# The same instruction streams behind an empty, closed tile context, instead of inside two critical sections of an open one

## The chip, the cores and the metric

The kernel runs on one core of a Trainium2 chip. The core has five engines with an instruction stream each: PE (matrix multiply), DVE (vector), ACT (scalar), POOL (general purpose) and SP (here it only issues DMAs and waits). The metric is the device time of one execution in microseconds. The kernel before was timed three times: 210.34, 210.49 and 210.49, median 210.49 us.

## What is computed

```python
batch, m, k, n = 16, 512, 1024, 768        # everything float32
x: [16, 512, 1024]   weight: [1024, 768]   bias: [768]   residual: [16, 512, 768]
out = np.matmul(x, weight) + bias + residual
```

As one product it has 8192 rows, cut into 64 tiles of 128 rows. Per tile the contraction of 1024 is eight steps of 128, and the 768 output columns are a part of 512 and one of 256.

## The kernel before, in words

**The work.** SP loads x and residual in pieces of several tiles into two large SBUF tensors (`X`, 16 tiles deep, and `R`, 32 tiles deep) and stores finished tiles from `R`. ACT casts an x tile to bf16 (`XB`). PE transposes it as four 128x128 blocks of 32-bit words (L335) into PSUM (`PT`), DVE copies that to SBUF (`XT`), and PE multiplies (weights L353, matmul L342) into one of three PSUM tiles (`PO`). DVE adds PSUM into the residual (L286), and POOL adds the bias (L286). Four tiles near the end are transposed by ACT and DVE instead (L297 to L331). At the start the weights are loaded, cast and kept, and PE runs dummy products (L397) on a zeroed tile before the first data land.

**The order.** Nothing is scheduled by a planner. The code calls `op(engine, emit, reads, writes)`, which appends to a list in `Program.add` (L59), and `ORDER` (L36) and `HEAD_ORDER` (L30) fix by hand what SP issues and how the first three tiles are interleaved. `Program.emit` (L72) works out from reads and writes which instruction must wait for which, gives each DMA a landing semaphore (`landed_0` and so on, L118), and emits each engine's stream with explicit waits (L134). For PE, the middle 54 tiles are a loop of nine turns with six tiles each (`Fori`, L160); its first instruction is placed at a fixed slot of a fetch block (`head_slot`).

**Around the streams.** The kernel runs inside `with TileContext(nc)` (L493). Memory comes from two tile pools, and semaphores from the tile context. The streams are emitted in a critical section (L461); behind them SP waits for the landings of all stores but the last four (L463). A second critical section, on SP alone (L465), has the waits for those four. What the tile framework puts around a critical section is not in the kernel's text: a NOP on SP at the start (L461), for which all engines wait in a branch (L493); after the first section a drain on each engine and SP's waits for them (L461); after the second a branch, an event, a drain and a NOP on SP (L493, L465); and at the end of the context two barriers of all engines with a clearing of semaphores between them (L493). A barrier is a drain on each engine that counts up a semaphore, POOL's wait for four of them, POOL's release, and each engine's wait for that release. One more such barrier stands at the very start (L482), from the making of the program itself, behind four small memsets on POOL.

Of the kernel before, what the change touches and what calls it, by code (L numbers as in the profile page):

```python
# [11 lines left out]
P = 128  # L12
QUAD = 32
# [26 lines left out]
 ('r', 2, 6, 16), ('s', 1, 0, 16), ('x', 3, 0, 6), ('r', 3, 0, 7), ('x', 3, 6, 16),  # L40
 ('r', 3, 7, 16), ('s', 2, 0, 16), ('s', 3, 0, 10), ('s', 3, 10, 13),
 ('s', 3, 13, 15), ('c', 3, 15, 0), ('c', 3, 15, 1)]
OUTSIDE = 4
LAST = [(0, 512), (512, 256)]


class Program:

    def __init__(self, tc):
        nc = tc.nc
        self.nc, self.tc = nc, tc
        self.engines = {"pe": nc.tensor, "dve": nc.vector, "act": nc.scalar, "pool": nc.gpsimd, "sp": nc.sync}
        self.ops, self.writer, self.readers = [], {}, {}
        self.form, self.kind = [], []

    def add(self, eng, emit, rd=(), wr=(), dma=False, kind=None):  # L59
        n, ops = len(self.ops), self.ops  # L60
        deps = {self.writer[k] for k in (*rd, *wr) if k in self.writer and (eng != "pe" or ops[self.writer[k]][0] != eng)}
        for k in wr:
            deps.update(d for d in self.readers.get(k, ()) if ops[d][0] != eng or ops[d][3])
        for k in rd:
            self.readers.setdefault(k, set()).add(n)
        for k in wr:
            self.writer[k], self.readers[k] = n, set()
        self.ops.append((eng, emit, deps - {n}, dma))
        self.form.append((tuple(rd), tuple(wr)))
        self.kind.append(kind or f"done_{eng}")  # L70

    def emit(self, ends, turns):  # L72

        ops, known = self.ops, {e: {} for e in self.engines}
        lane, count, snap, waits, slots, slot = [], {}, [], [], [], {}  # L80
        for n, (eng, _, deps, dma) in enumerate(ops):
            mine = (n, 0) if dma else (eng, count.setdefault(eng, 0) + 1)
            if not dma:
                count[eng] += 1
            seen = known[eng]
            need = {}
            for d in deps:
                f, i = lane[d]
                if seen.get(f, -1) < i and i > need.get(f, (-1, 0))[0]:
                    need[f] = (i, d)  # L90
            need = {
                f: (i, d) for f, (i, d) in need.items()
                if not any(snap[d2].get(f, -1) >= i for g, (_, d2) in need.items() if g != f)
            }
            for f, (i, d) in need.items():
                for g, v in (*snap[d].items(), (f, i)):
                    if seen.get(g, -1) < v:
                        seen[g] = v
            waits.append([d for _, d in need.values()])
            lane.append(mine)  # L100
            if dma:
                free = [i for i, used in enumerate(slots) if seen.get(used[-1], -1) >= 0]
                if not free:
                    free = [len(slots)]
                    slots.append([])
                slot[n] = free[0], len(slots[free[0]]) + 1
                slots[free[0]].append(n)
            own = dict(seen)
            own[mine[0]] = mine[1]
            snap.append(own)  # L110
        body = [[n for n in range(a, b) if ops[n][0] == "pe"] for a, b in zip(turns, turns[1:])]
        for same in zip(*body, strict=True):
            assert len({self.form[n] for n in same}) == 1, [self.form[n] for n in same]
        told = {d for w in waits for d in w}
        told |= {n for same in zip(*body) if told & set(same) for n in same}
        told |= {n for n, k in enumerate(self.kind) if not k.startswith("done_")}
        sems = {k: self.tc.alloc_semaphore(k) for k in dict.fromkeys(self.kind) if k != "done_sp"}
        landings = [self.tc.alloc_semaphore(f"landed_{i}") for i in range(len(slots))]  # L118
        total, mark = dict.fromkeys(sems, 0), {}
        for n, (eng, _, _, dma) in enumerate(ops):  # L120
            if dma:
                mark[n] = (landings[slot[n][0]], 16 * slot[n][1])
            elif n in told:
                total[self.kind[n]] += 1
                mark[n] = (sems[self.kind[n]], total[self.kind[n]])

        def put(n, e):
            ins = ops[n][1](e)
            if ops[n][3]:
                ins.then_inc(mark[n][0], 16)  # L130
            elif n in told:
                ins.then_inc(mark[n][0], 1)

        def straight(todo):  # L134
            for n in todo:
                e = self.engines[ops[n][0]]
                for d in waits[n]:
                    e.wait_ge(*mark[d])  # L138
                put(n, e)

        pe = self.engines["pe"]
        straight(n for n, op in enumerate(ops) if op[0] != "pe" or n < turns[0])
        at = {}
        for same in zip(*body):
            for j, n in enumerate(same):
                for d in waits[n]:
                    at.setdefault(same[0], {}).setdefault(self.kind[d], {})[j] = mark[d][1]
        first, step = {}, {}
        order = [(n, k, w) for n in body[0] for k, w in at.get(n, {}).items()]
        for k in dict.fromkeys(k for _, k, _ in order):  # L150
            mine = [w for _, g, w in order if g == k]
            n_w = len(mine)
            assert all(len(w) == len(body) for w in mine), (k, mine)
            flat = [w[j] for j in range(len(body)) for w in mine]
            assert flat == list(range(flat[0], flat[0] + len(body) * n_w)), (k, flat)
            first[k] = flat[0]
        reg = {k: pe.alloc_register(f"count_{k}") for k in first}
        for k, r in reg.items():
            pe.reg_mov(r, first[k])
        with self.nc.Fori(0, len(body), 1, engines=OrderedEngineSet([pe.engine]), head_slot={pe.engine: 32}):  # L160
            for n in body[0]:
                for k in at.get(n, {}):
                    pe.wait_ge(sems[k], reg[k])
                    pe.reg_add(reg[k], reg[k], 1)
                put(n, pe)
        straight(n for n, op in enumerate(ops) if op[0] == "pe" and n >= turns[-1])
        return [mark[n] for n in ends]
# [3 lines left out]
def kernel(  # L171
# [8 lines left out]
    nc = tc.nc  # L180
# [11 lines left out]
    out_d = out2d.rearrange("(S p j) n -> S p j n", p=P, j=J)  # L192
    w_d = weight.rearrange("(q p e) n -> p q e n", p=P, e=2)

    sb = ctx.enter_context(tc.tile_pool(name="sb", bufs=1))
    ps = ctx.enter_context(tc.tile_pool(name="ps", bufs=1, space=bass.MemoryType.PSUM))

    def fixed(pool, name, n, shape, dt):
        return [pool.tile(shape, dt, name=f"{name}", tag=f"{name}{i}", bufs=1) for i in range(n)]

    (X,) = fixed(sb, "x_tile", 1, [P, XR, K], FP32)
    (R,) = fixed(sb, "ro", 1, [P, RR, N], FP32)
    XB = fixed(sb, "xb", XB_N, [P, K], BF16)
    XT = fixed(sb, "xt", XT_N + 1, [P, n_q, P, 2], BF16)
    XD = fixed(sb, "xd", 2, [P, 2, n_q, P // QUAD, 2 * QUAD], BF16)
# [9 lines left out]
    prog = Program(tc)  # L215
# [5 lines left out]
    def dma(dst, src, rd, wr):  # L221
        op("sp", lambda e: e.dma_start(out=dst, in_=src), rd, wr, dma=True)  # L222
# [6 lines left out]
    stores = []  # L229

    def pump():
        while queue:
# [18 lines left out]
            queue.pop(0)  # L251
            t0, nj = J * S + j0, j1 - j0
            if kind == "b":
                dma(bias_row.rearrange("(g p) n -> g p n", p=QUAD)[:, 0, :],
                    bias[None, :].to_broadcast([P // QUAD, N]), [], ["bias_row"])
                continue
            if kind == "w":
# [20 lines left out]
    def mark(*what):  # L278
        done.add(what)
        pump()  # L280
# [128 lines left out]
    dummies(WARM, 0)  # L409

    pump()
    for kind, *a in HEAD_ORDER:
        if kind == "bias":
# [15 lines left out]
        else:  # L429
            mm_all(a[0], [a[1]])  # L430
    pump()
    for t in range(HEAD - 1):
        if ("fin", t) not in done:
# [3 lines left out]
    turns = []  # L437
# [20 lines left out]
    mark("out", t)  # L458
    pump()
    assert not queue, queue  # L460
    with tc.tile_critical():  # L461
        landed = prog.emit(stores, turns)
        for sem, value in landed[:-OUTSIDE]:  # L463
            nc.sync.wait_ge(sem, value)
    with tc.tile_critical(sync_engine=mybir.EngineType.SP):  # L465
        for sem, value in reversed(landed[-OUTSIDE:]):
            nc.sync.wait_ge(sem, value)


# [28 lines left out]
```

## Time and profile before

| what | value |
|---|---|
| median of three runs | 210.49 us |
| the profiled execution's own time | 210.39 us |
| its span, first to last instruction | 208.6 us |
| what lies around the span | 1.79 us |
| PE busy | 200.8 us (96%) |
| DMA | 87.10 MB, mean 418 GB/s |
| POOL, DVE, ACT busy | 115.2, 105.4, 82.5 us |
| mean granted PE clock | 0.992 |

A row of the profile's groups has the line, engine, operation and tile, then how often, busy time in all, mean of one, and the idle time ahead of it with what ended that. The chain of waits follows the last instruction back to what released it, step by step, and gives start and duration of each piece. The view of one line of the program lists every instruction that the line stands for, those too that only wait (EVENT_SEMAPHORE), drain or branch, with minimum, median and maximum of the duration in ns and the first and last start in us. "SPq" and the like are an engine's sequencer: an instruction that does no work on data.

### The profile page before, as it was taken

To read this page: it belongs to the slowest core of one execution; us is meant where nothing else is said; L and a number is where in the kernel's file an instruction comes from. 1 tells how busy PE (TensorE), PEld (TensorE's weight loads), DVE (VectorE), ACT (ScalarE), POOL (GpSimd) and SP (SyncE) were. 2 spreads that over 40 slices of the span, in tenths; PEclk is the share of its full clock that TensorE was granted. 3 is DMA by queue.
4 is the path that set the end of the run, shared out by engine and by line. 5 is a ranking of instruction groups with operands and counts; after the bars stand their busy time and mean duration, and the time that the engine had idled before them with its cause. 6 is when DMAs were issued, how large, how long until landed. Compare 5 with 4: busy or idle time off the path is not lost.

```text
span 208.6 us, 2622 instructions
## 1 busy us (share of the span) xinstructions
PE 200.8 (96%) x1282; PEld 79.6 (38%) x778; DVE 105.4 (51%) x141; ACT 82.5 (40%) x97; POOL 115.2 (55%) x71
## 2 busy tenths in 40 slices
PE   7999999999999999999999999999999999999980
PEld 2433433443443344344344434434443443443230
DVE  1448555445545543754454454555445545547460
ACT  2444513412731362340272074232074039999600
POOL 1100029759999804999019801999306960899200
PEclk9999999999999999999999999999999999999996
DMA  6999999899989899999999999999999999999983
GB/s 233 425 424 432 433 419 475 385 444 421 504 374 495 383 383 445 452 401 429 426 474 402 424 454 412 452 452 405 431 419 475 408 413 469 405 443 420 448 366 145
DMA packets 4621, 87.10 MB, mean 418 GB/s; under 512 B 516, under 2 KB 644, under 8 KB 1416
## 3 DMA queue, kind: packets, MB, share of 16 engines
q1 hardware_dynamic: 4616, 87.05, 97.8%
q8 instruction: 2, 0.03, 0.1%
q14 instruction: 3, 0.02, 0.0%
HBM read 61.88 MB, written 25.17 MB: 417 GB/s over the span
## 4 chain that ended last, share of the span: by engine, by line
PE 71%; DMA 23%; ACT 1%; DVE 1%; SPq 0%; issue 0%; ACTq 0%
PE psum_o L342 62%; DMA x_tile<-in_x_dram 23%; PE pt L335 10%; ACT xb L283 1%; SPq L222 0%; DVE xt L283 0%; DVE ro L286 0%; SPq L493 0%; ACTq L138 0%; SPq L461 0%
## 5 line engine op out<-in xcount | busy, mean ns | idle before, releaser
L342 PE MATMUL psum_o<-w_sb,xt 128*128 128x256 bf16 (+1 forms) x1024 | 176.0, 326 | 0.3 <-DVE xt L283 0.3
L286 POOL TENSOR_TENSOR ro<-ro,bias_sb 128x768 f32<-128x768 f32 x50 | 88.8, 1809 | 47.4 <-DMA ro<-in_residual_dram 47.4
L283 ACT CAST xb<-x_tile 128x1024 bf16<-128x1024 f32 (+1 forms) x59 | 58.0, 1022 | 108.7 <-DMA x_tile<-in_x_dram 59.4
L353 PEld LDWEIGHTS <-xt 128*128 128x128 bf16 x520 | 50.9, 98 | 103.5 <-issue 101.2
L283 DVE COPY xt<-pt 128x1024 bf16<-128x1024 bf16 x60 | 41.3, 691 | 78.0 <-PE pt L335 78.0
L286 DVE TENSOR_TENSOR ro<-psum_o,ro 128x768 f32<-128x768 f32 (+2 forms) x51 | 47.6, 933 | 8.2 <-POOL ro L286 5.1
L286 POOL TENSOR_TENSOR ro<-ro 128x768 f32<-128x768 f32 x14 | 24.9, 1815 | 25.1 <-DMA ro<-in_residual_dram 25.0
L335 PE MATMUL pt<-ident,xb 128*128 128x128 f32 x240 | 36.3, 276 | 0.2 <-ACT xb L283 0.2
L335 PEld LDWEIGHTS pt<-ident,xb 128*128 128x128 f32 x240 | 28.2, 142 | 14.8 <-issue 13.1
L283 ACT CAST xd<-x_tile 32x512 bf16<-32x512 f32 x32 | 19.7, 616 | 0.4
L286 DVE TENSOR_TENSOR ro<-psum_o,bias_sb 128x768 f32<-128x768 f32 x14 | 13.2, 949 | 0.0
L397 PE MATMUL psum_o<-warm 128*128 128x512 bf16 x18 | 6.9, 548 | 1.4 <-DVE warm_a L289 1.4
L283 ACT CAST w_sb<-ro 128x768 bf16<-128x768 f32 x4 | 3.3, 832 | 3.8 <-DMA ro<-in_weight_dram 3.8
L283 DVE CAST xb<-x_tile 128x512 bf16<-128x512 f32 (+1 forms) x4 | 1.9, 492 | 5.3 <-DMA x_tile<-in_x_dram 5.3
L328 DVE STREAM_TRANSPOSE xt<-xd 128x512 f32<-128x512 f32 x4 | 2.8, 704 | 3.0 <-ACT xd L283 3.0
L397 PEld LDWEIGHTS psum_o<-warm 128*128 128x128 bf16 x18 | 2.2, 130 | 4.6 <-issue 3.0
L283 POOL CAST w_sb<-ro 128x768 bf16<-128x768 f32 x1 | 0.8, 822 | 5.7 <-DMA ro<-in_weight_dram 5.7
L283 DVE CAST w_sb<-ro 128x768 bf16<-128x768 f32 x3 | 1.7, 558 | 2.0 <-DMA ro<-in_weight_dram 2.0
L283 ACT ACT_TABLE_LOAD x1 | 1.3, 1283 | 0.9 <-SPq L461 0.9
L414 DVE STREAM_SHUFFLE bias_sb<-bias_row 128x768 f32<-128x768 f32 x1 | 1.0, 1039 | 0.0
L289 DVE MEMSET warm<- 128x256 uint32 x1 | 0.3, 272 | 1.1 <-SPq L461 1.1
L289 DVE MEMSET bias_row<- 128x768 f32 x1 | 0.7, 698 | 0.2 <-issue 0.2
(9 smaller groups left out, 1.2 us busy)
## 6 DMA issues: line engine op xcount, KB each, us to landing
out_dram<-ro SPq DMA_DIRECT2D x3, 6144.0 KB, 34.6
x_tile<-in_x_dram SPq DMA_DIRECT2D x3, 5120.0 KB, 24.5
ro<-in_residual_dram SPq DMA_DIRECT2D x3, 3840.0 KB, 33.1
x_tile<-in_x_dram SPq DMA_DIRECT2D x3, 3072.0 KB, 33.9
ro<-in_residual_dram SPq DMA_DIRECT2D x3, 2304.0 KB, 18.5
x_tile<-in_x_dram SPq DMA_DIRECT2D x4, 1024.0 KB, 10.7
x_tile<-in_x_dram SPq DMA_DIRECT2D x2, 2048.0 KB, 23.2
out_dram<-ro SPq DMA_DIRECT2D x1, 3840.0 KB, 13.1
```

Source lines behind the costliest of these rows:

```text
L283: op(eng, lambda e: (e.copy if eng == "act" else e.tensor_copy)(out=dst, in_=src), rd, wr, kind=kind)
L286: op(eng, lambda e: e.tensor_add(out=dst, in0=a, in1=b), rd, wr)
L289: op(eng, lambda e: e.memset(dst, v), [], [wr])
L328: op("dve", lambda e: e.transpose(out=XT[slot(t)].rearrange("p q m e -> p (q m e)").bitcast(FP32), in_=XD[at][:, t - strips[t]].rearrange( ...
L335: op("pe", lambda e, q=q: e.transpose(out=pt[:, q, :], in_=words[:, ts(q, P)], identity=ident), [("XB", t % XB_N, 2 * q // n_q), "ident"], ...
L342: return e.add_instruction(mybir.InstMatmult(name=nc.get_next_instruction_name(), ins=[e.lower_ap(rhs), e.lower_ap(lhsT, for_matmul_weight ...
L353: op("pe", lambda g: g.ldweights(lhsT), rd)
L397: op("pe", lambda e: e.matmul(PO[i][:, 0:512], lhsT=warm[:, 0:P], rhs=warm, start=True, stop=True), ["warm"], [("PO", i)])
L414: op("dve", lambda e: e.stream_shuffle(out=bias_sb, in_=bias_row, mask=[0] * QUAD), ["bias_row"], ["bias"])
```

## The change

The tile context is closed before anything is put into it (`tc.close()`, `tc.compile()`), at the top of the kernel function. Memory and semaphores come from the program directly (`nc.alloc_sbuf_tensor`, `nc.alloc_psum_tensor`, `nc.alloc_semaphore`). Both critical sections go; the streams are emitted as they are, and SP ends with the waits for all stores in order of issue. The one DMA that loads the bias names its four target rows by a stride instead of by a rearranged view. Line numbers fall by 4 to 9.

```diff
-OUTSIDE = 4
...
-        sems = {k: self.tc.alloc_semaphore(k) for k in dict.fromkeys(self.kind) if k != "done_sp"}
-        landings = [self.tc.alloc_semaphore(f"landed_{i}") for i in range(len(slots))]
+        sems = {k: self.nc.alloc_semaphore(k) for k in dict.fromkeys(self.kind) if k != "done_sp"}
+        landings = [self.nc.alloc_semaphore(f"landed_{i}") for i in range(len(slots))]
...
-    sb = ctx.enter_context(tc.tile_pool(name="sb", bufs=1))
-    ps = ctx.enter_context(tc.tile_pool(name="ps", bufs=1, space=bass.MemoryType.PSUM))
-
-    def fixed(pool, name, n, shape, dt):
-        return [pool.tile(shape, dt, name=f"{name}", tag=f"{name}{i}", bufs=1) for i in range(n)]
+    tc.close()
+    tc.compile()
+    sb, ps = nc.alloc_sbuf_tensor, nc.alloc_psum_tensor
+
+    def fixed(alloc, name, n, shape, dt):
+        return [alloc(f"{name}{i}", shape, dt).ap() for i in range(n)]
...
-                dma(bias_row.rearrange("(g p) n -> g p n", p=QUAD)[:, 0, :],
+                dma(bias_row[0:P:QUAD, :],
                     bias[None, :].to_broadcast([P // QUAD, N]), [], ["bias_row"])
...
-    with tc.tile_critical():
-        landed = prog.emit(stores, turns)
-        for sem, value in landed[:-OUTSIDE]:
-            nc.sync.wait_ge(sem, value)
-    with tc.tile_critical(sync_engine=mybir.EngineType.SP):
-        for sem, value in reversed(landed[-OUTSIDE:]):
-            nc.sync.wait_ge(sem, value)
+    for sem, value in prog.emit(stores, turns):
+        nc.sync.wait_ge(sem, value)
```

In the built programs, the instructions that do work are the same ones in the same order on every engine, with the same operands, the same SBUF and PSUM addresses and the same semaphore numbers. What differs:

| place | before | after |
|---|---|---|
| start, each engine | the first barrier, then SP's NOP and a branch that waits for it | the first barrier, then the closed context's two barriers |
| after the streams | one drain per engine and SP's waits for them, four empty or waiting branches | nothing |
| end of SP | last store's wait, branch, event, drain, NOP, two barriers | last store's wait |
| semaphores | cleared between the two last barriers | not cleared by the program |
| PE instructions ahead of the loop | 214 | 217 |

## The prediction

> **What bounds the kernel now.** I began with the page: the busy shares, the slices over time, and the DMA queue.
>
> ```profile
> PE 200.8 (96%) x1282; PEld 79.6 (38%) x778; DVE 105.4 (51%) x141; ACT 82.5 (40%) x97; POOL 115.2 (55%) x71
> ...
> PE   7999999999999999999999999999999999999980
> ...
> DMA  6999999899989899999999999999999999999983
> ...
> q1 hardware_dynamic: 4616, 87.05, 97.8%
> q8 instruction: 2, 0.03, 0.1%
> ```
>
> PE and the DMA queue are both full from the second slice to the last but one. PE's own view of waits sums to 1.9 us, 1.4 of it ahead of the first dummy product; behind that PE waits 0.3 us for a copy out of PSUM (DVE xt L283) and 0.2 for a cast. So the middle has no slack in either resource, and no empty place for an edit to hide in. But the change leaves the middle alone: the built programs have the same working instructions, operands, addresses and semaphores on every engine. What it touches is the first microsecond and the last one and a half. The chain of waits shows the first:
>
> ```profile
> 0.67 0.05 issue
> 0.72 0.01 SPq L461
> 0.73 0.06 issue
> 0.80 0.03 SPq L493
> 0.83 0.12 issue
> 0.95 0.39 SPq L222
> 1.33 0.06 issue
> 1.39 0.41 SPq L222
> ...
> 1.85 7.98 DMA x_tile<-in_x_dram
> ```
>
> Columns are start, duration, what. The program's first barrier has released SP at 0.67. Then SP runs the NOP of the critical section (L461) and the branch into it (L493), and issues its first load at 0.95. Two DMA issues in a row on SP are 0.06 apart. The third load, issued at 1.85, lands at 9.83, and from then on the pieces are PE almost alone up to 202.70, but for a DMA from 63.19 to 103.06 that PE had nearly caught up with. All of that hangs on waits and has no date of its own: if SP, DVE, ACT and PE all start d later, I expect everything up to the last store d later.
>
> The end is in the view of line L493, taken between 207.0 and 207.42, and then between 207.4 and 208.7:
>
> ```profile
> L493 SPq EVENT_SEMAPHORE  x2: 287/446/605, 206.5 to 207.1; - x2
> L493 SPq COMPARE_BRANCH  x1: 33/33/33, 207.4 to 207.4; - x1
> ```
>
> ```profile
> L493 POOLq EVENT_SEMAPHORE  x4: 17/17/17, 207.9 to 208.5; - x4
> L493 SPq DRAIN  x3: 7/7/7, 207.8 to 208.1; - x3
> L493 SPq EVENT_SEMAPHORE  x2: 17/17/17, 208.0 to 208.5; - x2
> ...
> L493 PEldq EVENT_SEMAPHORE  x2: 51/51/51, 208.0 to 208.6; - x2
> L493 POOLq DRAIN  x2: 34/64/94, 208.0 to 208.3; - x2
> ...
> L493 POOLq EVENT_SEMAPHORE_RANGE_CLEAR  x1: 160/160/160, 208.2 to 208.2; - x1
> L493 PEldq DRAIN  x1: 8/8/8, 208.2 to 208.2; - x1
> ```
>
> SP's last wait for a landing starts at 207.1 and lasts 287 ns (605 would run past the branch at 207.4): the output is complete at 207.4. The other 1.2 us up to 208.6 are bookkeeping: the branch out of the section, its event, drain and NOP (207.4 to 207.8), a barrier (207.8 to 208.0), the clearing of the semaphores (160 ns) and a second barrier (up to 208.6).
>
> **The change part by part.**
>
> *The end: −1.2 us.* The changed program ends at SP's wait for the last store: 208.6 − 207.4 = 1.2 us go from the span. Nothing is late next: the other engines have nothing left, PE's last matmul being over at 202.7. What goes behind the first section (drains, waits and NOPs at 203.9 to 204.7) is worth nothing: SP then waits for landings until 207.4 in any case, and that wait is the cover. The new order of the waits costs nothing for the same reason: four wait instructions at the 0.05 to 0.07 us that such ones are apart are done long before 207.4, and the last to be satisfied is still the last store.
>
> *The start, taken out: −0.2 us.* Between SP's release (0.67) and its first issue (0.95) lie 0.28; a plain step between two instructions of SP is 0.06; so NOP and branch are worth 0.28 − 0.06 = 0.22. At least nothing, if the first issue costs its own 0.15 behind anything. I take 0.2.
>
> *The start, put in: +0.7 us.* The closed context leaves its two barriers, with no clearing between them since it has used no semaphore. The nearest row is the pair at the end: PE passes one release at 208.0 and the next at 208.6, SP at 208.0 and 208.5, so 0.55 from release to release, and that includes the 0.16 of clearing and a drain more on POOL (34 ns and a step, 0.05). That leaves 0.34. It can be built from the other side too: PE passes at 208.0 and drains at 208.2, 0.2 later, and POOL's two events need 0.16 after that (four of them from 207.9 to 208.5, in pairs 0.08 apart): 0.36. I take 0.35 a barrier, 0.7 for two. Bounds: 0.2 below (SP's drain at 207.8 to its release at 208.0) and 0.55 above (the clearing counted in). Queued behind these waits is everything: the table load on ACT, the zeroing of the dummies' operand on DVE and so PE's dummies, and on SP all loads. SP's first load decides, since the DMA queue is full from there on.
>
> *Memory, semaphores, the bias DMA: 0.* Same addresses and numbers, and the bias DMA has the same four rows of 768. Nothing covers this, nothing needs to: there is no difference to time.
>
> *Around the span: 0.* The profiled execution took 210.39 us for a span of 208.6, so 1.79 lie outside. Nothing in the trace shows what they are. Four engines now end 4 to 5 us ahead of SP instead of with it. If all of the 1.79 were work of those four at their end, it could go; if something outside has to make up for the barrier and the clearing that the program leaves out, it could grow by the 0.8 us that they take now (207.8 to 208.6). I take no change.
>
> On this the Trainium skill has a rule, in "Runtime: NRT & Kernel Launch", section "The launch sequence": behind every kernel the runtime runs a barrier of all engines and a reset of the semaphores. By this, neither an early end of four engines nor the missing clear would change what lies outside, and the sum stays as it is; no trace here shows it.
>
> *Sum.* −1.2 − 0.2 + 0.7 = −0.7 us. On the profiled execution 210.39 − 0.7 = 209.69, so **209.7 us**. The median shown, 210.49, lies 0.10 above that execution; from it the sum gives 209.8. The parts' bounds give −1.2 − 0.22 + 2 × 0.2 = −1.0 and −1.2 − 0 + 2 × 0.55 = −0.1, that is 209.4 to 210.3. About 0.2% (0.42 us, up to 210.07) is what a measurement here can tell from no change.
>
> **A second rule against the row: the clock.** Twelve dummies occupy 1.40 to 6.70 (0.44 each), three later ones 0.81 (0.27): PE's clock rises between 6.49 and 7.72. If the rise came 1 us later against the data, PE would do 0.5 us less by then, of which its 0.27 wait for the copy takes up a half: +0.2. The three timed runs lie within 0.15 us, so whatever moves there moves little. "TensorE: Matmul & The Clock Gate", section "Part 1: The HAM clock gate (the "warmup" mystery)", says that the full clock comes after a busy window of about 3.4 us, and that the windows run free of the kernel's start. By this the later start of PE could meet another phase, and the rise come up to 6.8 us after the first dummy, where the row has 5.1 to 6.3: up to 1.7 us later, 0.85 less the 0.27, so +0.6 by the rule and a sum of −0.1. I stay with the row.
>
> **The rivals.**
>
> *A, the forecast*, 209.7: the end gives 1.2, the start takes 0.5 back.
>
> *B, more goes: 209.2.* The four engines' early end takes a part of the 1.79 with it. For: they stand 4 to 5 us in a barrier now that need not be there. Against: SP, the last, still has its own end ahead of it. Taking a quarter, 0.45: 210.39 − 0.7 − 0.45 = 209.2.
>
> *C, no gain worth the name: 210.3.* The start's barriers cost their upper bound, because at the start the engines do not arrive together (drains of the first barrier from 0.0 on SP to 0.3 on PE) and nothing of NOP and branch is won back: 210.39 − 0.1. That the change does not do what it says belongs here: if the closing barrier and clear are only moved outside, the 0.8 come back, and 210.39 − 0.7 + 0.8 = 210.5.
>
> *D, slower: 211.4.* PE has 217 instructions ahead of the loop instead of 214, and the loop's first instruction stands at a fixed slot of a fetch block. If the three more pass that slot, the loop moves a whole block on, and PE's branch into it (170 to 223 ns now, the loop's branches on line L160) has to wait for that block. The page counts two instruction fetches on q8 with 0.1% of 16 engines' span: 0.001 × 16 × 208.6 / 2 = 1.7 us each, 0.8 to 2.5 within its rounding; the longest the trace would support is the 4.2 us that the last small store takes to land. PE has no slack behind 22 us, so all of it shows: 210.39 − 0.7 + 1.7 = 211.4 (210.5 to 213.9). It decides from 0.7 us of stall on. For: a fixed slot must overflow somewhere. Against: 3 slots in a block of 256 are a small target.
>
> **How the numbers follow.** A 0.74, B 0.10, C 0.11, D 0.05. A and B are faster by more than 0.2%: 0.84. C is the same: 0.11. D is slower: 0.05. The range takes in A's bounds and C's 210.3 at the top and reaches past B's 209.2 to 209.0 at the bottom; D and the last part of C are left out.
>
> **What would show it.** In the profile after: SP's first load issued at about 1.4 instead of 0.95, ahead of it two barriers 0.35 apart; ACT's table load and DVE's first memset 0.4 to 0.5 later; the third load's landing, PE's last matmul and the last landing all about 0.5 later; the span ending with a wait of SP, at about 207.9. B would show as a span of 207.9 with less than 1.7 around it; C as a first load at 1.9 or later, or more around the span; D as idle time of PE at about 22 us. I am wrong in the reasoning, not only in a size, if the middle (from the third load's landing to PE's last matmul) gets longer or shorter by more than 0.2 us.

## The result, and the profile after

The changed kernel took 209.16 us in the median of six runs (208.97 to 209.31), the kernel before 210.49 (210.02 to 210.68). The ratio is 0.9938, with a 95% interval of 0.9926 to 0.9951: 1.33 us less. The forecast was 209.7, in a range of 209.0 to 210.3. Direction and range hold; the gain is about twice the 0.7 that the sum gave, and the difference has one place.

| | before | after | change |
|---|---|---|---|
| profiled execution, us | 210.39 | 209.13 | −1.26 |
| its span | 208.6 | 207.8 | −0.8 |
| around the span | 1.79 | 1.33 | −0.46 |
| first load issued | 0.95 | 1.38 | +0.43 |
| third load landed | 9.83 | 10.34 | +0.51 |
| PE's last product done | 202.70 | 203.09 | +0.39 |
| from the last landing's wait to the end of the span | 1.2 | 0 | −1.2 |

The page first. Rows of busy time, the slices and the queues stand almost as they were. PE's busy time is 1.8 us lower, but PE did not have less work: 1002 of the 1024 records of the main product are in this trace (176.0 us busy before, 174.8 after), and the dummy products, the same 18, took 6.2 us instead of 6.9 because the clock rose earlier among them.

```profile
PE 199.0 (96%) x1260; PEld 78.9 (38%) x778; DVE 105.3 (51%) x141; ACT 82.5 (40%) x97; POOL 115.2 (55%) x71
...
PE   6989999999999999999999999999999999999990
...
DMA  5999999999998999989999899989999999998996
...
q1 hardware_dynamic: 4616, 87.05, 98.2%
q8 instruction: 2, 0.03, 0.1%
```

The start, in the chain of waits of the kernel after (start, duration, what):

```profile
1.32 0.06 issue
1.38 0.39 SPq L218
...
2.29 8.05 DMA x_tile<-in_x_dram
```

SP issues its first load one step of 0.06 behind its release at 1.32; NOP and branch are gone. The release comes late because of the closed context, line L191 (instruction, how often, min/median/max ns, first and last start):

```profile
L191 POOLq EVENT_SEMAPHORE  x4: 17/17/17, 0.9 to 1.3; - x4
...
L191 SPq EVENT_SEMAPHORE  x2: 17/17/17, 1.0 to 1.3; - x2
...
L191 PEldq EVENT_SEMAPHORE  x2: 51/51/51, 1.0 to 1.3; - x2
```

Two releases, at 1.0 and 1.3, where the first barrier's was at 0.7: (1.32 − 0.67) / 2 = 0.33 for each barrier. The end, in the chain and in the view of the line with SP's waits, taken from 207.5 to 208:

```profile
199.56 3.54 PE psum_o L338 x21
203.09 0.02 issue
203.12 0.42 DVE ro L282
```

```profile
L458 SPq EVENT_SEMAPHORE  x1: 28/28/28, 207.8 to 207.8; - x1
```

The last store is waited for until 207.8, and that is the end of the span. What the table follows in between is 0.4 to 0.5 later than before. So the span did what the sum said, 0.8 against 0.7; the other 0.46 come from what lies around the span, where I had put nothing.

### The profile page after: what moved, and what is told of

It reads as the page before. It is cut to its first block, busy times and chain, and to the rows that moved or that the text cites. A ratio compares the mean times of both kernels' runs of the same rounds, so it can differ in the third digit from the quotient of the medians.

```text
span 207.8 us, 2574 instructions
## 1 busy us (share of the span) xinstructions
PE 199.0 (96%) x1260; PEld 78.9 (38%) x778; DVE 105.3 (51%) x141; ACT 82.5 (40%) x97; POOL 115.2 (55%) x71
## 4 chain that ended last, share of the span: by engine, by line
PE 91%; DMA 4%; issue 1%; DVE 1%; SPq 0%; ACT 0%
PE psum_o L338 79%; PE pt L331 12%; DMA x_tile<-in_x_dram 4%; SPq L218 0%; DVE xt L279 0%; ACT xb L279 0%; DVE ro L282 0%
## 5 line engine op out<-in xcount | busy, mean ns | idle before, releaser
L338 PE MATMUL psum_o<-w_sb,xt 128*128 128x512 bf16 (+1 forms) x1002 | 174.8, 325 | 1.7 <-DVE xt L279 0.3
L393 PE MATMUL psum_o<-warm 128*128 128x512 bf16 x18 | 6.2, 503 | 1.8 <-DVE warm_a L285 1.8
```

The costliest lines, as they stand in the source:

```text
L338: return e.add_instruction(mybir.InstMatmult(name=nc.get_next_instruction_name(), ins=[e.lower_ap(rhs), e.lower_ap(lhsT, for_matmul_weight ...
L393: op("pe", lambda e: e.matmul(PO[i][:, 0:512], lhsT=warm[:, 0:P], rhs=warm, start=True, stop=True), ["warm"], [("PO", i)])
```

## The experiments

For every single run, the execution's time and the span are known (the span to 0.1), so the time around it is a mean over a kernel's runs. It was 1.785 to 1.793 for the kernel before in all three groups of experiments (13 to 24 runs each) and 1.335 for the kernel after (six runs, 1.30 to 1.37). The theory: four engines now end well before SP, and whatever an engine does behind its last instruction is then done while SP still waits. How far before is not the 4 to 5 us of the prediction for all four: PE (203.09) and DVE (203.54) end 4.7 and 4.3 us ahead of SP's 207.8, but ACT and POOL 11 and 13 us, as their last rows in the timeline after show (start, duration, what):

```profile
189.74 6.89 ACT L279 CAST xd<-x_tile 32x512 bf16<-32x512 f32 x11
189.34 5.38 POOL L282 TENSOR_TENSOR ro<-ro,bias_sb 128x768 f32<-128x768 f32 x3
```

The rival: the part that shrank belongs to the closing barriers and the clearing of semaphores that the program no longer has.

**1. All engines end together again** (e1_end_together).

```diff
-    for sem, value in prog.emit(stores, turns):
+    landed = prog.emit(stores, turns)
+    for sem, value in landed:
         nc.sync.wait_ge(sem, value)
+    for e in (nc.tensor, nc.vector, nc.scalar, nc.gpsimd):
+        e.wait_ge(*landed[-1])
```

> The changed kernel, but PE, DVE, ACT and POOL also wait for the landing of the last store, so that all five engines end together, with no barrier and no clearing. Theory (the 0.46 us by which the time around the span fell, from 1.79 to 1.33, belongs to four engines that now end early): the span stays at 207.8, the time around it goes back to about 1.8, the execution takes about 209.6. Rival (it belongs to the barriers and the clearing that are gone, whenever the engines end): span 207.8, around 1.3, execution 209.15 as now.

Measured: 209.75 us (ratio to before 0.9972, 0.9961 to 0.9982), span of the profiled run 207.8, around 1.81 in the mean of eight runs. The view of the four added waits (L461):

```profile
L461 ACTq EVENT_SEMAPHORE  x1: 17/17/17, 207.8 to 207.8; - x1
L461 POOLq EVENT_SEMAPHORE  x1: 17/17/17, 207.8 to 207.8; - x1
L461 DVEq EVENT_SEMAPHORE  x1: 21/21/21, 207.8 to 207.8; - x1
L461 PEldq EVENT_SEMAPHORE  x1: 51/51/51, 207.8 to 207.8; - x1
```

The waits end with SP's at 207.8, so the span has not moved; no barrier and no clearing has come back, and the 0.46 have. The rival falls.

**2. No tile context at all** (e2_no_context). The kernel function is called with a plain object that holds `nc`.

```diff
-    tc.close()
-    tc.compile()
...
-    with _tile.TileContext(nc) as tc:
-        tile_matmul_bias_add_kernel(tc, *args)
+    tile_matmul_bias_add_kernel(_Plain(nc=nc), *args)
```

> The changed kernel without any tile context, so without the two barriers that the closed one leaves at the start. Theory (each of them delays everything by 0.33 us, and nothing in between takes it up): SP's first load at 0.72 instead of 1.38, span 207.15, around 1.33, execution about 208.5. Rival (the middle is held by something with a date of its own, or the first fetches of instructions are the limit): less than 0.3 us gained, execution 208.9 or more.

Measured: 208.56 us (ratio 0.9917, 0.9903 to 0.9932), around 1.33. SP's issues in order of time, and its last wait:

```profile
0.73 0.39 SPq L216 DMA_DIRECT2D x_tile<-in_x_dram  x1
```

```profile
L456 SPq EVENT_SEMAPHORE  x1: 28/28/28, 207.2 to 207.2; - x1
```

The first load goes 0.65 earlier than in the kernel after (1.38), and the last landing is 0.6 earlier. A delay at the start reaches the end undiminished. This version beats both kernels: 1.8 us less than before.

**3. Two more barriers at the start** (e3_four_barriers).

```diff
     tc.close()
     tc.compile()
+    nc.all_engine_barrier()
+    nc.all_engine_barrier()
```

> The changed kernel with two more barriers at the start, four in all behind the first. Theory (0.33 us each, passed on in full): first load at 2.04, span 208.45, around 1.33, execution about 209.8. Rival (barriers overlap with something else at the start, so that more of them cost less or more than the first two): execution under 209.5 or over 210.1.

Measured: 209.93 us (ratio 0.9979, 0.997 to 0.9988), around 1.32, and in the chain:

```profile
2.08 0.39 SPq L220
...
2.98 8.12 DMA x_tile<-in_x_dram
```

2.08 − 1.38 = 0.70 for two, against 0.65 for the two of experiment 2. The price of a barrier at the start is 0.33 to 0.35, whichever ones are counted.

**4. Two barriers at the end** (e4_end_barriers).

```diff
     for sem, value in prog.emit(stores, turns):
         nc.sync.wait_ge(sem, value)
+    nc.all_engine_barrier()
+    nc.all_engine_barrier()
```

> The changed kernel with two barriers of all engines behind the waits for the stores, as before but with no clearing between them. Theory (an end of all engines together costs 0.46 outside, and each barrier 0.2 to 0.35 inside): span about 208.4, around 1.8, execution about 210.2. Rival (the time around the span depends on the clearing of the semaphores, not on who ends when): span about 208.4, around 1.33, execution about 209.75.

Measured: 210.31 us (ratio 0.9995, 0.9986 to 1.0004: no difference from before), around 1.80. The lines of the two barriers, L459 and L460:

```profile
L459 SPq DRAIN  x1: 13/13/13, 208.0 to 208.0; - x1
...
L459 SPq EVENT_SEMAPHORE  x1: 17/17/17, 208.1 to 208.1; - x1
```

```profile
L460 SPq EVENT_SEMAPHORE  x1: 17/17/17, 208.5 to 208.5; - x1
```

The wait for the last store in this run ends at 207.9, so the first barrier, at which the others stand ready, takes 0.2 and the second 0.3; a span 0.65 longer in the median of the runs, and 0.46 more around it. With two barriers at its end, even without the clearing, the changed kernel has no gain left that can be told from none: the whole gain is in the end (1.2 + 0.46 = 1.66), and the start gives back about a quarter of it (0.43). The rest of the old end (branch, event, drain, NOP and clearing, 1.2 − 0.65 = 0.55) was not put back by any run.

**5 to 8. Which engine's end counts** (e5_pe_too, e6_dve_too, e7_act_too, e8_pool_too). Experiment 1 with one engine alone in the place of the four:

```diff
+    for e in (nc.tensor,):
+        e.wait_ge(*landed[-1])
```

> The changed kernel, but PE too waits for the landing of the last store, so that PE and SP end last. The span stays at 207.8. Theory (every engine has closing work of its own, and the 0.46 us are the slowest of them, PE, which was the last to arrive at each barrier): around 1.8, execution 209.6. Rival (all engines are collected one after the other, so the cost is spread): around 1.45, execution 209.3.

> The same with DVE in the place of PE. Theory (PE's closing is the slowest): around 1.33 to 1.45, execution 209.2. Rival (spread over the engines): around 1.45, execution 209.3.

> The same with ACT. Theory (PE's closing is the slowest): around 1.33 to 1.45, execution 209.2. Rival (spread over the engines): around 1.45, execution 209.3.

> The same with POOL. Theory (PE's closing is the slowest): around 1.33 to 1.45, execution 209.2. Rival of its own (POOL's is the slowest, since its drains are the longest, 34 to 94 ns against 7 to 10): around 1.8 here and 1.33 with PE.

| ends last, with SP | runs | execution, us | around, mean | lowest to highest |
|---|---|---|---|---|
| none (the kernel after) | 6 | 209.16 | 1.33 | 1.30 to 1.37 |
| DVE | 3 | 209.42 | 1.43 | 1.42 to 1.44 |
| ACT | 4 | 209.49 | 1.49 | 1.48 to 1.50 |
| PE | 4 | 209.56 | 1.58 | 1.55 to 1.61 |
| POOL | 8 | 209.86 | 1.86 | 1.82 to 1.91 |
| all four (experiment 1) | 8 | 209.75 | 1.81 | 1.77 to 1.86 |

My choice, PE as the slowest, is wrong, and so is an even spread; the rival written for POOL is right on POOL, but had 1.33 for PE, which reads 1.58. As to a sum over the engines: the four excesses over 1.33 are 0.10, 0.16, 0.25 and 0.53, which add up to 1.04, while all four together cost 0.48. A maximum fits that, a sum does not. POOL alone accounts for the whole of it. That POOL alone reads 0.05 above all four together is mostly a matter of where the span ends. In the profile of experiment 1 the span ends with PE's wait of 51 ns, 0.04 behind POOL's; counted from the end of POOL's own last instruction, the rest of the execution is 1.85 us there and 1.86 in experiment 8. The kernel before fits as well: its POOL ends 0.09 ahead of the span, and 1.78 + 0.09 = 1.87.

**9 and 10. POOL a little earlier** (e9_pool_second, e10_pool_third). POOL waits for an earlier store.

```diff
     for e in (nc.gpsimd,):
-        e.wait_ge(*landed[-1])
+        e.wait_ge(*landed[-2])     # e10: landed[-3]
```

> The changed kernel, but POOL too waits for the last store but one, which lands 0.32 us ahead of the last. Theory (what lies around is the longest of the engines' closings, counted from where each ends, POOL's 1.86 against SP's 1.33): around 1.86 - 0.32 = 1.54, execution 209.4. Rival (POOL's wait costs its 0.5 whenever it stands late in the program): around 1.86, execution 209.7.

> The changed kernel, but POOL too waits for the last store but two, which lands 0.95 us ahead of the last. Theory (the longest of the closings): POOL is done before SP, around 1.33, execution 209.2. Rival (a fixed cost of a late POOL): around 1.86, execution 209.7.

Measured: 209.33 us (0.9943, 0.9915 to 0.9971), around 1.52 in six runs; and 209.32 (0.9933, 0.9898 to 0.9969), around 1.32 in five. POOL's wait in the two, with SP's last at 208.0 in both:

```profile
L461 POOLq EVENT_SEMAPHORE  x1: 17/17/17, 207.7 to 207.7; - x1
```

```profile
L461 POOLq EVENT_SEMAPHORE  x1: 17/17/17, 207.0 to 207.0; - x1
```

With POOL 0.3 ahead of SP its 1.86 shows as 1.52; with POOL a whole microsecond ahead SP's own 1.32 is left. Counted from POOL's last instruction, the 1.52 are 1.86 again in the profile. So the time around the span behaves as the longest of the engines' closings, each counted from that engine's own last instruction. For PE and ACT this was measured only with the wait for the last store.

**11. The waits on DVE instead of SP** (e11_dve_alone).

```diff
     for sem, value in prog.emit(stores, turns):
-        nc.sync.wait_ge(sem, value)
+        nc.vector.wait_ge(sem, value)
```

> The changed kernel with the waits for all stores on DVE instead of SP; SP ends with the issue of the last store, at about 204.2. Theory (the longest of the closings; DVE and SP together gave 1.43, SP alone 1.33): around 1.43, execution 209.25. Rival (the two closings share a step, and DVE alone would be shorter than SP): around under 1.33, execution under 209.15, which would be a better place for the waits.

Measured: 209.43 us (0.9944, 0.9921 to 0.9968), around 1.43 in six runs. The end of the span is now DVE's:

```profile
L458 DVEq EVENT_SEMAPHORE  x4: 50/50/50, 205.1 to 207.9; - x4
```

The same 1.43 as with DVE and SP together: SP's part does not matter when it is the shorter one. Of the two engines tried alone in this place, SP is the better one.

## Why the prediction held, and where it did not

*The end, −1.2.* Right: the span ends with SP's wait for the last landing, and nothing came in the place of what was there.

*The start, −0.2 and +0.7, together +0.5.* Right in both terms, a little high: NOP and branch went (the first load stands 0.06 behind SP's release, as taken), and a barrier costs 0.33, where 0.35 was taken. Together +0.43. Experiments 2 and 3 show the price by taking barriers away and by adding some.

*The middle shifts as a whole.* Right: from the third load's landing to PE's last product it is 203.09 − 10.34 = 192.75 us, before 202.70 − 9.83 = 192.87, within the 0.2 that I had set. Experiments 2 and 3 move the start by −0.65 and +0.70, and the median span follows with −0.65 and +0.80.

*Around the span, 0.* Wrong, and the one step of the sum that failed: the term was put at 0 because the trace does not show what lies there. I took no change, between a loss of 0.8 and a gain of at most 1.79. It was −0.46. Rival B named the mechanism and the size (0.45, by taking a quarter, which was a guess and not a derivation), and I gave it 0.10 against the forecast's 0.74. My argument against B, that SP "still has its own end ahead of it", treats all ends as equally long. Experiments 5 to 10 show that they are not: POOL's is 0.53 longer than SP's, so with POOL away from the end SP's shorter one is what is left. The sum with this term is −1.2 + 0.43 − 0.46 = −1.23, against −1.26 measured on the profiled executions.

That the range held is therefore partly luck. The bounds of the sum's own parts ended at 209.4, above the 209.16 that was measured; the range holds it only because it was drawn down to 209.0 for the sake of B.

*The rule on what lies outside.* The Trainium skill, "Runtime: NRT & Kernel Launch", section "The launch sequence", has a barrier of all engines and a reset of semaphores behind the kernel; from that I drew that an early end of four engines could not matter. Experiment 1 shows that it does, by 0.48. What stands outside in detail, no trace here shows; a maximum over engines would fit with some work per engine ahead of a common wait, but that is argued, not shown.

*The clock rule.* The trace before had twelve dummies in 5.30 us; after, PE's timeline has

```profile
1.84 4.63 PE L393 MATMUL psum_o<-warm 128*128 128x512 bf16 x12 [1.84 <-DVE warm_a L285]
6.72 1.09 PE L331 MATMUL pt<-ident,xb 128*128 128x128 f32 x8 [0.25 <-DVE xb L279]
```

so here the rise came earlier in the dummies; in experiment 1 they took 4.22 us, in experiments 2 and 3 5.30 again. Its place against the kernel's start does wander; the Trainium skill, "TensorE: Matmul & The Clock Gate", section "Part 1: The HAM clock gate (the "warmup" mystery)", says that the clock's windows run free of that start. The earlier rise won nothing, since PE then waited 0.25 for data. By the granted clock in the thirteen profiles the rise came 2.7 to 6.0 us after the first dummy. The rise at up to 6.8 us, which the prediction estimated from that page and which would cost, is in none of them, and was not tried.

*C and D* did not happen: the barriers cost 0.33 at the start, not 0.55, the time around the span did not grow, and PE shows no stall at the loop: its branch into the loop took 176 ns, before 170, and it has no wait over 0.3 us behind the dummies.

## What to carry to other kernels

The time of a kernel is more than its span. In these runs it is as if each engine had a closing time behind its last instruction, counted from where that engine ends, of which only the longest shows; what an engine does in it is not in the traces. So let no engine wait at the end that need not, POOL least of all, and put the last wait on SP (1.33 us behind it, 1.43 behind DVE alone). In this kernel, which is full from its first load to its last store, two barriers of all engines cost 0.65 to 0.70 us at the start and 0.65 of span at the end. An empty framework context is not free: it costs two of them. The changed program also leaves its semaphores uncleared, and no trace here shows who clears them.

## What the runs showed of the hardware that was not expected

The time outside the span depends on which engine ends last: 1.33 us with SP alone, 1.43 with DVE, 1.49 with ACT, 1.58 with PE, 1.86 with POOL. It did not depend on barriers or on the clearing of semaphores in the program: with all engines ending together it is 1.81 without either, 1.80 with barriers alone, and 1.79 with both.
